# A transformer block on one core: memory attention's rows kept on chip, norms beside the last product, sums kept for the tail

## The chip, the core and the metric

One core of a Trainium2 chip runs the whole program in one launch. TensorE (PE) multiplies and transposes, VectorE (DVE), ScalarE (ACT) and GpSimd (POOL) do the elementwise work, SyncE (SP) issues most transfers, and 16 DMA engines carry them out. The metric is the device time of one execution in microseconds; the kernel before has three timed runs and one profiled execution.

## The reference, cut to what matters

`x` has 1024 rows of 1024. The block adds three terms to it, one after the other; a mixer with two kinds of sparse attention stands ahead of what the change touches.

```python
x = x + hybrid_mixer(rms_norm(x, norm1_g), ...)            # its last product is o @ w_out
x = x + memory_xattn(rms_norm(x, norm2_g), mem, ...)
x = x + square(relu(rms_norm(x, norm3_g) @ w_ff_in)) @ w_ff_out

def memory_xattn(h, mem, ...):                             # 4 heads of 128, 256 memory rows
    q = rms_norm(h @ w_xq); k = rms_norm(m @ w_xk); v = m @ w_xv
    o = softmax(q k^T * 128 ** -0.5) v                     # [1024, 512]
    return o @ w_xo
```

## The kernel before

**Tiles.** The 1024 rows are eight tiles of 128. A product needs its left operand transposed, features on the partitions. Most products split an operand into a high and a low part of a rounded format (`split_w`, L248, and `split_ps`, L242) and add three products; others take whole float32 operands, and such a product has two records in the trace.

**Stages.** `project` makes the projections of tiles 0 to 3 and then 4 to 7. After that two streams are mixed by `together` (L114): `attend`, the sparse attention tile by tile, and `fill` (L1219), which holds all other work: the second half of the projections, `memory` (keys and values of the memory), `between` for tiles 0 and 1, `between` for 2 and 3, `mlp` for tiles 0 to 3, and `between` for 4 and 5. When attention is done, `merge` (L1248) mixes what is left of `fill` with `between` for tiles 6 and 7, and `mlp_tail` (L1078) does the MLP of tiles 4 to 7.

**`between` (L919)** takes two tiles. It loads the attention outputs `o` and the rows of `x`, adds `o @ w_out` to them (four chunks of 256 columns, `gemm`, L322), normalizes and transposes the sums (`norm_T2`, L298: a square with row sums on ScalarE, a power on GpSimd, two scalings on VectorE, eight transposes on TensorE), and makes the queries in two chunks of 256 columns, two heads each. After a chunk, `memory_item` (L956) runs for both tiles in turns, a step of one and then of the other: norm of the queries, transposes, scores, softmax, transposes, values. Its result `o`, 128 rows by 256 columns, is written to a DRAM tensor `xo` (L1003). When both chunks are done, each tile's 512 columns are read back (L1009), transposed in one group of four (`to_T`, L276) into `xf`, and multiplied by `w_xo` in four chunks, each added to the sums. With `keep` the sums stay in SBUF (`x2s`), else they are written to `x2_dr` (L1017).

**The MLPs.** `mlp` (L1019) loads the sums of tiles 0 and 1 from `x2_dr`, normalizes and transposes all four tiles one after the other, and then goes through eight groups of 512 features. `mlp_tail` does the same for tiles 4 to 7; its first `G` = 2 groups run for tiles 4 and 5 before the norms of 6 and 7 (L1152). Tiles 4 and 5 come from `x2_dr` by `start` (L1086).

**Buffers.** `RINGS` (L38) gives the number of buffers of each tag in each pool. In `dn`, the pool of the middle, `b4` has four of 128x1024, `wraw` two (weights as loaded), `relu` two. `res` holds four rows of sums for the tail. A new tile takes a buffer that is free, and its first writer waits until the last reader of the old one is done. `psM`, where transposes land, has one buffer in the main part.

**Order.** Python makes the instructions in one order. A scheduler then orders each engine's queue by its own model of times (`TC_ARGS`, L83), so that instructions of the two streams alternate on every engine. Each engine, and SP with its transfers, works through its queue in that order: an instruction that waits holds up those behind it.

## Time and profile before

| | |
|---|---|
| timed runs, median of three (lowest, highest) | 1804.89 us (1802.81, 1807.52) |
| the profiled execution's own time | 1801.23 us |
| its span, first to last instruction | 1799.5 us |
| mean granted TensorE clock | 0.978 |
| busy: TensorE, its weight loads | 1697.9, 1460.7 us |
| busy: DVE, ACT, POOL | 948.0, 1070.5, 882.3 us |
| HBM read, written | 170.98, 20.97 MB |

A row of a timeline begins with its start in us from the span's first instruction and how long it took; `[1.82 <-DMA relu<-xo]` at its end says that the engine sat idle for 1.82 us before it, and what ended the wait. `psD<-whi,b` reads: written tile, read tiles. `psS`, `psPT` and `psPV` belong to attention in the main part and to the `between` of tiles 6 and 7 after it, `psD` and `psM` to `fill` and the tail. In the table by stage each engine has its busy time and its instructions, then come the granted TensorE clock as a share of full speed, the share of the DMA engines and the rate. SPq is SP's queue, with the time that issuing took. The program orders, of which the prediction speaks too, hold no times: they list each engine's instructions in the order of its queue, for the kernel before and the changed one.

### The profile page before, as it was taken

To read this page: it belongs to the slowest core of one execution; us is meant where nothing else is said; L and a number is where in the kernel's file an instruction comes from. 1 tells how busy PE (TensorE), PEld (TensorE's weight loads), DVE (VectorE), ACT (ScalarE), POOL (GpSimd) and SP (SyncE) were. 2 spreads that over 40 slices of the span, in tenths; PEclk is the share of its full clock that TensorE was granted. 3 is DMA by queue.
4 is the path that set the end of the run, shared out by engine and by line. 5 is a ranking of instruction groups with operands and counts; after the bars stand their busy time and mean duration, and the time that the engine had idled before them with its cause. 6 is when DMAs were issued, how large, how long until landed. Compare 5 with 4: busy or idle time off the path is not lost.

```text
span 1799.5 us, 28038 instructions
## 1 busy us (share of the span) xinstructions
PE 1697.9 (94%) x9326; PEld 1460.7 (81%) x9326; DVE 948.0 (53%) x2397; ACT 1070.5 (59%) x2687; POOL 882.3 (49%) x1025
## 2 busy tenths in 40 slices
PE   6989999899998889999998999999999889999998
PEld 6987988788787778778886888888978778888887
DVE  4556767667864675274564565656623552222223
ACT  4444885895697569845797457994512543333333
POOL 2356545564541446468476577563211444444445
PEclk9999999899999999999999999999999899999999
DMA  7334222654344311212222122225374642333333
GB/s 200 114 133 114 64 62 75 203 140 151 100 147 157 87 33 54 69 59 79 60 75 75 59 68 65 68 84 183 98 250 145 212 128 84 96 94 97 95 121 106
DMA packets 176977, 193.80 MB, mean 108 GB/s; under 512 B 25664, under 2 KB 144192, under 8 KB 176832
## 3 DMA queue, kind: packets, MB, share of 16 engines
q1 hardware_dynamic: 168896, 181.52, 33.3%
q0 software_dynamic: 7936, 10.49, 2.2%
q8 instruction: 74, 1.21, 0.3%
q14 instruction: 71, 0.58, 0.1%
HBM read 170.98 MB, written 20.97 MB: 107 GB/s over the span
## 4 chain that ended last, share of the span: by engine, by line
PE 69%; DMA 8%; DVE 8%; ACT 6%; POOL 4%; issue 4%; SPq 1%; POOLq 0%; DVEq 0%; ACTq 0%
PE psD L224 49%; PE psS L224 8%; PE psPV L224 4%; PE psPT L719 4%; ACT dmask L660 2%; POOL wlo L257 2%; PE psM L282 1%; DMA wraw<-in_w_ff_out_dram 1%; DMA xo<-relu 1%; POOL S L709 1%; DMA wraw<-in_w_ff_in_dram 1%; DMA qin<-q 1%; DMA x<-b 1%; DVE S L702 1%; ACT whi L252 1%
## 5 line engine op out<-in xcount | busy, mean ns | idle before, releaser
L257 POOL TENSOR_TENSOR wlo<-wraw,whi 128x512 fp32r<-128x512 f32 (+1 forms) x225 | 305.6, 1363 | 283.3 <-ACT whi L252 278.8
L224 PE MATMUL psD<-whi,h 128*128 128x512 f32 x1024 | 343.1, 403 | 10.3 <-DVE b L1148 5.4
L252 ACT ACTIVATE whi<-wraw 128x512 fp32r<-128x512 f32 x321 | 200.3, 627 | 208.2 <-PE psD L224 156.9
L224 PEld LDWEIGHTS psD<-whi,h 128*128 128x128 f32 x1024 | 194.0, 191 | 55.4 <-DVE b L1148 8.8
L224 PE MATMUL psD<-xh,whi 128*128 128x512 f32 (+1 forms) x576 | 211.3, 371 | 3.5 <-ACT relu L1051 2.6
L224 PE MATMUL psD<-xh,wlo 128*128 128x512 f32 (+1 forms) x576 | 211.6, 369 | 0.0
L224 PE MATMUL psD<-xl,whi 128*128 128x512 f32 (+1 forms) x576 | 211.0, 369 | 0.0
L224 PE MATMUL psD<-wlo,h 128*128 128x512 f32 x512 | 203.9, 399 | 0.6 <-POOL wlo L257 0.6
L224 PE MATMUL psD<-whi,xh 128*128 128x256 f32 (+1 forms) x704 | 194.2, 358 | 1.4 <-DVE Vd L244 0.9
L224 PE MATMUL psD<-wlo,xh 128*128 128x256 f32 (+1 forms) x704 | 191.2, 353 | 2.7 <-DMA wlo<-in_w_in_dram 2.3
L244 DVE TENSOR_TENSOR pl<-psPT,ph 128x512 fp32r<-128x512 f32 (+1 forms) x232 | 142.4, 620 | 62.0 <-ACT ph L243 61.0
L704 ACT ACTIVATE S<-S,mn 128x128 f32<-128x128 f32 (+7 forms) x192 | 142.8, 745 | 53.8 <-DVE mn L702 53.0
L243 ACT ACTIVATE ph<-psPT 128x512 fp32r<-128x512 f32 (+1 forms) x232 | 122.9, 540 | 65.3 <-PE psPT L719 57.9
L709 POOL TENSOR_SCALAR S<-S,sums,gi 128x640 f32<-128x640 f32 (+7 forms) x128 | 107.9, 852 | 108.7 <-DVE sums L707 81.2
L257 DVE TENSOR_TENSOR wlo<-wraw,whi 128x512 fp32r<-128x512 f32 (+1 forms) x96 | 82.9, 863 | 148.3 <-ACT whi L252 148.2
L224 PEld LDWEIGHTS psD<-wlo,xh 128*128 128x128 f32 x704 | 132.6, 194 | 14.3 <-DMA wlo<-in_w_in_dram 2.7
L224 PEld LDWEIGHTS psD<-whi,xh 128*128 128x128 f32 x704 | 133.2, 197 | 12.0 <-DVE Vd L244 1.5
L719 PE MATMUL psPT<-c_ident,S 128*128 128x128 f32 x816 | 132.5, 279 | 4.7 <-POOL S L709 2.3
L224 PEld LDWEIGHTS psD<-xh,whi 128*128 128x128 f32 x576 | 108.3, 188 | 21.5 <-ACT relu L1051 3.5
L224 PEld LDWEIGHTS psD<-xl,whi 128*128 128x128 f32 x576 | 108.2, 188 | 17.8
L224 PEld LDWEIGHTS psD<-xh,wlo 128*128 128x128 f32 x576 | 108.4, 188 | 17.5 <-POOL wlo L257 0.3
L224 PE MATMUL psS<-K,qh 128*128 128x384 f32 (+3 forms) x288 | 110.5, 387 | 4.4 <-DVE mn L702 3.7
(286 smaller groups left out, 3843.9 us busy)
## 6 DMA issues: line engine op xcount, KB each, us to landing
wraw<-in_w_ff_in_dram SPq DMA_DIRECT2D x40, 512.0 KB, 4.0
wraw<-in_w_ff_out_dram SPq DMA_DIRECT2D x40, 512.0 KB, 3.8
wraw<-in_w_ff_in_dram SPq DMA_DIRECT2D x64, 256.0 KB, 2.8
wraw<-in_w_ff_out_dram SPq DMA_DIRECT2D x64, 256.0 KB, 2.7
whi<-in_w_out_dram SPq DMA_DIRECT2D x32, 256.0 KB, 4.1
wlo<-in_w_out_dram SPq DMA_DIRECT2D x32, 256.0 KB, 4.3
wraw<-in_w_in_dram SPq DMA_DIRECT2D x24, 256.0 KB, 3.8
q<-st SPq DMA_DIRECT2D x12, 512.0 KB, 2.9
```

Source lines behind the costliest of these rows:

```text
L224: te.matmul(o, a, b, start=start, stop=stop)
L243: s.activation(hi, src, AF.Copy)
L244: v.tensor_tensor(lo, src, hi, op=ALU.subtract)
L252: s.activation(hi, raw, AF.Copy)
L257: (v if l == "v" else g).tensor_tensor(lo, raw, hi, op=ALU.subtract)
L282: te.transpose(pt[:, j, :], x_t[:, (c + j) * P:(c + j + 1) * P], ident)
L660: s.activation(mask, src, AF.Sign, bias=c, accum_out=over)
L702: v.tensor_tensor_reduce(out=dst, in0=sp, in1=m, scale=1.0, scalar=mn[:, 0:1] if i else 3e38, op0=ALU.add, op1=ALU.min, accum_out=low)
L704: s.activation(S, S, AF.Exp, bias=low, scale=-1.0, accum_out=sums[:, hh:hh + 1])
L709: g.tensor_scalar(Ss[hh], Ss[hh], sums[:, hh:hh + 1], 1.0 if gate is None else gate[:, hh:hh + 1], op0=ALU.mult, op1=ALU.mult)
L719: te.transpose(p2[:, j, hh, :], S[:, (c + j) * P:(c + j + 1) * P], ident)
```

## The change

Four edits. `memory_item` no longer writes `xo`: after a step's pause it transposes its 128x256 result at once, in two transposes, into a tile `xo` in SBUF (a buffer of `b4`), from which the `w_xo` product reads. `between` for tiles 2 and 3 gets a second stream, `pre_norms`, that alternates with its `w_xo` product: it loads the sums of tiles 0 and 1 from `x2_dr` (tile 1 in two halves that lie in `wraw`), normalizes and transposes them; `mlp` then only has tiles 2 and 3 to do, and loads tile 1 once more for the sums. If the pool `res` exists when `between` for tiles 4 and 5 comes to its `w_xo` product, its sums go to buffers of `res` and no longer through `x2_dr`. The tail's two rows of gains move to `res` and are loaded when that pool is opened.

```diff
...
     "p1": {"x4": 5, "st": 2, "relu": 4, "wraw": 4, "whi": 6, "wlo": 6, "c8": 4, "c4": 2, "kraw": 5, "pc": 2},
     "p2": {"x4": 5, "st": 1, "relu": 2, "whi": 4, "wlo": 4, "c8": 3, "c4": 1, "kraw": 4, "pc": 2},
     "dn": {"b4": 4, "h": 8, "relu": 2, "wraw": 2, "whi": 4, "wlo": 4},
-    "res": {"b4": 4},
+    "res": {"b4": 4, "g": 2},
     "d2": {"b4": 2, "h": 8, "relu": 2, "whi": 4, "wlo": 4},
-    "d3": {"g": 2, "h": 16, "relu": 2, "wraw": 4, "whi": 10, "wlo": 10},
+    "d3": {"h": 16, "relu": 2, "wraw": 4, "whi": 10, "wlo": 10},
 }
 PSUMS = {"p1": {"D": 4, "M": 3, "C": 1}, "main": {"S": 2, "PT": 2, "PV": 1, "D": 2, "M": 1}}
 TAGS = {"p1": ("D", "M", "C"), "p2": ("D", "M", "D"), "dn": ("D", "M"), "d2": ("S", "PT"), "d3": ("D", "M")}
...
     KX = [[dr.tile([P, 2, 256], F32R, tag=f"KX{a}{c}", name=f"KX{a}{c}") for c in range(2)] for a in range(2)]
     VX = [[dr.tile([P, 2, 256], F32R, tag=f"VX{a}{c}", name=f"VX{a}{c}") for c in range(2)] for a in range(2)]
     x2_dr = [dr.tile([P, DM], F32, tag=f"x2{t}", name=f"x2{t}") for t in range(NT)]
-    xo_dr = [dr.tile([P, 512], F32, tag=f"xo{t}", name=f"xo{t}") for t in range(NT)]
 
 
     ahead = {0: late["x"]}
...
             v.tensor_tensor(dst, pt, dst, op=ALU.add)
         return add_to
 
-    def between(pool, t0, nt, x2s, keep, res=None):
+    def between(pool, t0, nt, x2s, keep, res=None, then=None):
 
         o_of = []
         for t in range(nt):
...
         x2 = [ring(res or pool, "b4", [P, DM]) for t in range(nt)]
         for t in range(nt):
             nc.sync.dma_start(x2[t], I["x"][0, (t0 + t) * P:(t0 + t + 1) * P, :])
-        add_to = residual_add(x2)
-        four = [[(c * 256, 256)] for c in range(4)]
+        add_to, four = residual_add(x2), [[(c * 256, 256)] for c in range(4)]
         yield from gemm(pool, [lambda t, k: o_of[t][:, k, :]], 8, nt, W["w_out"], four, add_to)
         _, xf, xt_of = xT(pool, nt, True)
 
...
             yield 1.0
 
         kx, pts = [], {}
+        xo = ring(pool, "b4", [P, 4, nt * P])
 
         def consume_q(ci, t, pt):
             if t == 0:
...
             v.reciprocal(sums, sums)
             o = ring(pool, "relu", [P, 2, P])
             v.tensor_tensor(o, pv, sums[:, :, None].to_broadcast([P, 2, P]), op=ALU.mult)
-            nc.sync.dma_start(xo_dr[t0 + t][:, ci * 256:(ci + 1) * 256], o.rearrange("p h d -> p (h d)"))
+            yield 1
+            to_T(pool, o.rearrange("p h d -> p (h d)"), [xo[:, ci * 2:ci * 2 + 2, t * P:(t + 1) * P]], 2)
 
         yield from gemm(pool, xf, 8, nt, W["w_xq"], [[(0, 256)], [(256, 256)]], consume_q)
 
-        for t in range(nt):
-            o = ring(pool, "relu", [P, 512])
-            nc.sync.dma_start(o, xo_dr[t0 + t])
-            to_T(pool, o, [x[:, 0:4] for x in xt_of(t)], 4)
-            yield 0.5
-        yield from gemm(pool, xf, 4, nt, W["w_xo"], four, add_to)
+        if not keep and "res" in late:
+            kept = [ring(late["res"], "b4", [P, DM]) for t in range(nt)]
+            x2s.update((t0 + t, kept[t]) for t in range(nt))
+
+            def add_to(ci, t, pt):
+                cs = slice(ci * 256, (ci + 1) * 256)
+                v.tensor_tensor(kept[t][:, cs], pt, x2[t][:, cs], op=ALU.add)
+        last = gemm(pool, [lambda t, k: xo[:, k, t * P:(t + 1) * P]], 4, nt, W["w_xo"], four, add_to)
+        yield from alternate(last, then()) if then else last
         for t in range(nt):
             if keep:
                 x2s[t0 + t] = x2[t]
-            else:
+            elif t0 + t not in x2s:
                 nc.sync.dma_start(x2_dr[t0 + t], x2[t])
 
-    def mlp(pool, t0, nt, x2s):
+    def pre_norms(pool, made, x2s):
+
+        made["x"] = xT(pool, 4)
+        made["g"] = gain2(pool, W["norm3_g"])
+        xt_of = made["x"][2]
+        x2s[0] = ring(pool, "b4", [P, DM])
+        nc.sync.dma_start(x2s[0], x2_dr[0])
+        norm_T2(pool, x2s[0], made["g"], xt_of(0))
+        yield 1.0
+        halves_ = []
+        for c in range(2):
+            halves_.append(ring(pool, "wraw", [P, 512]))
+            nc.sync.dma_start(halves_[c], x2_dr[1][:, c * 512:(c + 1) * 512])
+        xs = xt_of(1)
+        ss = [small(pool, "nss", 1) for _ in range(2)]
+        for c in range(2):
+            s.activation(xs[0][:, c * 4:c * 4 + 4], halves_[c].rearrange("p (k c) -> p k c", c=P), AF.Square, accum_out=ss[c])
+        v.tensor_tensor(ss[0], ss[0], ss[1], op=ALU.add)
+        r = rsqrt_of(pool, ss[0], DM, 1, "n")
+        yield 0.5
+        for c in range(2):
+            xn = ring(pool, "relu", [P, 512])
+            v.scalar_tensor_tensor(xn, halves_[c], r[:, 0:1], made["g"][c], op0=ALU.mult, op1=ALU.mult)
+            to_T(pool, xn, [x[:, c * 4:c * 4 + 4] for x in xs], 4)
+            yield 0.5
+
+    def mlp(pool, t0, nt, x2s, made):
         x2 = []
         for t in range(nt):
             if t0 + t not in x2s:
...
                 nc.sync.dma_start(x2s[t0 + t], x2_dr[t0 + t])
             x2.append(x2s[t0 + t])
         add_to = residual_add(x2)
-        (xh, xl), _, xt_of = xT(pool, nt)
-        gb3 = gain2(pool, W["norm3_g"])
-        for t in range(nt):
-            norm_T2(pool, x2[t], gb3, xt_of(t))
+        (xh, xl), _, xt_of = made["x"]
+        for t in range(2, nt):
+            norm_T2(pool, x2[t], made["g"], xt_of(t))
             yield 1.0
 
         for f4 in range(8):
...
                                           x2[t][:, c * 512:(c + 1) * 512])
                     yield 2.6
 
-    def mlp_tail(pool, res, x2s, t0):
+    def mlp_tail(pool, res, x2s, t0, gb3):
 
         x2 = {}
         (xh, xl), _, xt_of = xT(pool, 4)
-        gb3 = [ring(pool, "g", [P, 512]) for _ in range(2)]
-        for i, gb in enumerate(gb3):
-            nc.sync.dma_start(gb, row(W["norm3_g"][i * 512:(i + 1) * 512]).to_broadcast([P, 512]))
 
         def start(t):
             if t0 + t in x2s:
...
     dn_pool = tc.tile_pool(name="dn", bufs=1, reuse_waits="tile")
     aw = aw_pool.__enter__()
     projected = []
+    late["x2s"] = {}
 
     def fill():
         for part in range(1, len(PARTS)):
...
         yield 1, PACES[1]
         yield from between(dn, 0, 2, {}, False)
         yield 3, PACES[2]
-        x2s = {}
-        yield from between(dn, 2, 2, x2s, True)
+        x2s, made = {}, {}
+        yield from between(dn, 2, 2, x2s, True, None, lambda: pre_norms(dn, made, x2s))
         yield 3, PACES[3]
-        yield from mlp(dn, 0, 4, x2s)
+        yield from mlp(dn, 0, 4, x2s, made)
         yield 5, PACES[4]
-        yield from between(dn, 4, 2, {}, False)
+        yield from between(dn, 4, 2, late["x2s"], False)
 
     rest = fill()
     together(attend(aw, st), rest, projected)
...
     sp_pool.__exit__(None, None, None)
     at_pool.__exit__(None, None, None)
     res_pool = tc.tile_pool(name="res", bufs=1, side="right", reuse_waits="tile")
-    res = res_pool.__enter__()
+    res = late["res"] = res_pool.__enter__()
+    gb3 = [ring(res, "g", [P, 512]) for _ in range(2)]
+    for i, gb in enumerate(gb3):
+        nc.sync.dma_start(gb, row(W["norm3_g"][i * 512:(i + 1) * 512]).to_broadcast([P, 512]))
     d2_pool = tc.tile_pool(name="d2", bufs=1, side="right", reuse_waits="tile")
     plan["w"] = PLAN_TAIL
     d2 = d2_pool.__enter__()
-    x2s = {}
+    x2s = late["x2s"]
     rest = (w for w in rest if not isinstance(w, tuple))
     merge((rest, REST), (between(d2, 6, 2, x2s, True, res), 45.0))
     dn_pool.__exit__(None, None, None)
     d2_pool.__exit__(None, None, None)
     with tc.tile_pool(name="d3", bufs=1, reuse_waits="tile") as d3:
-        mlp_tail(d3, res, x2s, 4)
+        mlp_tail(d3, res, x2s, 4, gb3)
     res_pool.__exit__(None, None, None)
     ctx.close()
 
```

## The prediction, made before the result was known

> **What bounds the kernel now.** I read the page's busy times first, then its chain of work, then the busy times by stage.
>
> ```profile
> PE 1697.9 (94%) x9326; PEld 1460.7 (81%) x9326; DVE 948.0 (53%) x2397; ACT 1070.5 (59%) x2687; POOL 882.3 (49%) x1025
> PE 69%; DMA 8%; DVE 8%; ACT 6%; POOL 4%; issue 4%; SPq 1%; POOLq 0%; DVEq 0%; ACTq 0%
> ```
>
> TensorE is the bound: busy 94% of the span and 69% of the chain. An edit that leaves its products alone (the program orders of both kernels hold 8460 products, of the same sizes) can only win the rest: time in which TensorE sits idle, and time at a lowered clock. The stages say where these are. I cut them at the places where the two program orders meet or part.
>
> ```profile
> core 0: us, PE busy (x) PEld busy (x) DVE busy (x) ACT busy (x) POOL busy (x), PEclk, DMA share, GB/s
> 473.00:568.00 95.00, 89.20 (x519) 78.75 (x518) 57.62 (x162) 79.91 (x216) 35.77 (x52) 0.98 0.46 142
> 568.00:592.00 24.00, 18.32 (x91) 14.27 (x91) 17.27 (x59) 15.41 (x44) 3.10 (x5) 0.93 0.29 101
> 592.00:686.00 94.00, 82.66 (x505) 71.33 (x505) 70.61 (x208) 62.59 (x154) 40.02 (x53) 0.96 0.20 58
> 686.00:760.00 74.00, 71.62 (x351) 58.88 (x350) 27.72 (x65) 64.09 (x159) 44.47 (x48) 0.98 0.22 67
> 760.00:1306.00 546.00, 532.06 (x2832) 451.23 (x2832) 313.62 (x746) 372.67 (x827) 325.67 (x330) 0.99 0.27 82
> 1306.00:1323.00 17.00, 14.43 (x64) 12.06 (x62) 2.62 (x6) 2.36 (x7) 3.17 (x6) 0.80 0.90 280
> 1323.00:1355.00 32.00, 31.50 (x160) 27.83 (x161) 10.07 (x30) 5.87 (x16) 1.94 (x3) 1.00 0.68 215
> 1355.00:1407.00 52.00, 44.63 (x250) 39.06 (x249) 25.70 (x64) 18.63 (x44) 11.02 (x14) 0.92 0.63 196
> 1407.00:1465.00 58.00, 57.59 (x365) 52.57 (x364) 25.37 (x37) 29.19 (x60) 30.13 (x32) 0.98 0.48 143
> 1465.00:1800.00 335.00, 320.52 (x1487) 264.52 (x1485) 95.67 (x130) 112.69 (x193) 151.42 (x128) 0.99 0.33 101
> ```
>
> A stage's loss is its length less the busy time, plus its length times the missing clock. 592 to 686 (end of the second `between`, norms of the MLP) loses 11.3 + 3.8 = 15.1 us. 1306 to 1323 (attention's end) loses 2.6 + 3.4 = 6.0 us. 1355 to 1407 (memory attention of tiles 6 and 7 and the tail's first norms) loses 7.4 + 4.2 = 11.5 us. The change works in these three and at one wait near 507. Up to 473 the order of the products is the same, and from 1465 on (the tail's MLP) it is the same again: nothing is to be won there.
>
> **The change part by part. (a) The detour through DRAM.** The four waits that it leaves on TensorE:
>
> ```profile
> 509.14 0.63 PE L282 MATMUL psM<-c_ident,relu 128*128 128x128 f32 x4 [1.82 <-DMA relu<-xo]
> 626.84 0.63 PE L282 MATMUL psM<-c_ident,relu 128*128 128x128 f32 x4 [3.32 <-DMA relu<-xo]
> 1363.46 0.66 PE L282 MATMUL psM<-c_ident,relu 128*128 128x128 f32 x4 [1.26 <-DMA relu<-xo]
> 1423.93 0.63 PE L282 MATMUL psPT<-c_ident,relu 128*128 128x128 f32 x4 [0.30 <-DMA relu<-xo]
> ```
>
> The bracket is the idle time and what ended it: 1.82 + 3.32 + 1.26 + 0.30 = 6.7 us over the four calls of `between`. The 24 transfers go; the 32 transposes of 128x128 stay 32, and ScalarE copies 16 half-size tiles in place of 8. In the changed order 19 to 40 products stand, in the two calls beside attention, between the last product of an item and the transposes of its result, so nothing is late in their place. First term, for the wait at 507: **-1.8**. The other three lie in the stages below and are counted there. One thing follows: `xo` sits in a `b4` buffer, so that the loads of tile 3's attention output wait for the first `w_xo` product to end, where they now trickle in early. The order leaves 25 products before their first use; I take 0, with 4 us as the far end (the wait of 3.32 is the nearest row for a transfer that comes late).
>
> **(b) Norms beside `w_xo`.** Now the MLP's eight groups of transposes stand with attention alone beside them, after all 32 `w_xo` products. In the changed order four of the eight stand among the `w_xo` products, and the first MLP product comes 93 products sooner. I take half of the stage's loss: **-7.6**, from 0 to -15.1. Not all of it, since the norms of tiles 2 and 3 still wait for the last `w_xo` sums.
>
> [...]
>
> **(c) The tail.** Tiles 4 and 5 stay in `res`: their trip through DRAM goes, and their norms and first features now stand beside the memory attention of 6 and 7, which today runs bare:
>
> ```profile
> 1402.16 1.22 PE L224 MATMUL psS<-h 128*128 128x256 f32 x4 [1.89 <-DVE h L244]
> 1405.38 0.48 PE L989 MATMUL psPT<-c_ident,relu 128*128 128x128 f32 x1 [1.99 <-ACT relu L983]
> ```
>
> In the changed order 75 feature products stand between the first scores of tiles 6 and 7 and their last `pv`. Of the 11.5 us I leave 3.5 (four norms now come at once on ScalarE and VectorE): **-8.0**, from 0 to -11.5. That tiles 4 and 5 really are kept is seen in the order: two writes of `x2_dr` are left of four.
>
> **(d) Attention's end, the other way.** The chunk of queries that fills TensorE today after attention's last product has mostly moved before it: 8 of its 16 products are left.
>
> ```profile
> 1306.13 0.28 PE L224 MATMUL psPV<-pl,Vd 128*128 128x256 f32 x1
> 1307.43 0.44 PE L224 MATMUL psD<-h 128*128 128x128 f32 x2 [1.02 <-ACT h L243]
> 1308.57 3.93 PE L224 MATMUL psD<-h 128*128 128x128 f32 x22
> 1312.30 2.02 PE L224 MATMUL psD<-whi,xh 128*128 128x256 f32 x4
> 1318.24 1.03 PE L224 MATMUL psD<-whi,xh 128*128 128x256 f32 x4
> 1323.08 1.10 PE L224 MATMUL psS<-whi,b 128*128 128x256 f32 x4 [1.22 <-DMA whi<-in_w_out_dram]
> 1302.31 2.47 SPq L925 DMA_DIRECT2D b<-o  x5
> 1308.45 0.58 SPq L733 DMA_DIRECT2D o<-oc  x1
> 1309.08 5.55 SPq L925 DMA_DIRECT2D b<-o  x11
> 1314.73 0.85 SPq L929 DMA_DIRECT2D b<-in_x_dram  x2
> 1316.89 0.38 SPq L273 DMA_DIRECT2D whi<-in_w_out_dram  x1
> ```
>
> Today, counted from 1306.1: last output written at +2.3, 11 loads of it in 5.55 us (0.50 each; 5 went earlier, and the 11 stood behind that write on SP, which issues in order), `w_out` asked for at +10.8, its first product at +17.0. In the changed queue of SP, all 16 loads of `o` stand behind four `w_xo` loads whose buffers are freed only by those last 8 query products. These take 8 x 0.45 = 3.6 us (a product is two records here; four records in 0.86 to 1.03 us), so the queue moves on at about +5, the 16 loads take 8.1, `w_out` is asked for at +13.1 and arrives 6.2 later: +19.3. TensorE has 3.6 us of queries and 12 scores, 12 transposes and 24 narrow products (0.18 at the lowered clock by the row of 22), some 10 us in all. So 9.3 us idle and again 3.4 of clock, 12.7 against 6.0: **+6.7**, from +2 (the loads go faster) to +12.
>
> **(e) The long stretch between.** Every edit also reshuffles what comes after it: 686 to 1306 holds the same products in another mix. Today it loses 3.9 + 19.4 = 23.3 us, by its two rows above. In the changed order attention is up to 78 products further behind, and its longest pause, for a top-k mask, has 108 MLP products alone in it, not 132. No row prices another mix; I take **0**, with 5 us to each side, about a fifth of the loss.
>
> Sum: -1.8 - 7.6 - 8.0 + 6.7 + 0 = -10.7. The profiled execution took 1801.23 us (span 1799.5), 3.7 less than the median of the three timed runs, 1804.89. So 1790.5 for a profiled execution like that one, and **1794** for the median.
>
> **The rivals.**
>
> *Both gaps close.* If (b) and (c) win nearly all (-13, -11) and (d) costs 3, the sum with (a) is -23: 1782. For it: today's gaps there are latencies, and the new order puts products into them. Against it: (d).
>
> *The gain moves.* (b) wins 3, since tiles 2 and 3 wait as before, (c) 5, (a) nothing, as the loads of tile 3 come late, and (d) costs 9: +1, 1806. For it: in 1306 to 1323 DMA is already at 0.90 of its engines, so earlier requests need not land earlier. [...]
>
> *Slower: the MLP starts without weights.* `pre_norms` holds tile 1 in both `wraw` buffers of `dn` until its norm is done, so the MLP's first four weight loads can start only then.
>
> ```profile
> 638.83 0.38 SPq L262 DMA_DIRECT2D wraw<-in_w_ff_in_dram  x1
> 643.96 5.83 SPq L262 DMA_DIRECT2D wraw<-in_w_ff_in_dram  x2
> 656.16 0.37 SPq L262 DMA_DIRECT2D wraw<-in_w_ff_in_dram  x1
> 686.05 0.40 PE L224 MATMUL psD<-xh,whi 128*128 128x512 f32 x1
> L252 ACT ACTIVATE whi<-wraw 128x512 fp32r<-128x512 f32 x321 | 200.3, 627 | 208.2 <-PE psD L224 156.9
> wraw<-in_w_ff_in_dram SPq DMA_DIRECT2D x64, 256.0 KB, 2.8
> L257 POOL TENSOR_TENSOR wlo<-wraw,whi 128x512 fp32r<-128x512 f32 (+1 forms) x225 | 305.6, 1363 | 283.3 <-ACT whi L252 278.8
> ```
>
> Today the first goes 47 us before the first MLP product. From the first request to the fourth it takes 17.3 us, and with landing (2.8) and the two splits (0.6 and 1.4) 22 us until the fourth is ready. In the changed order about 90 products lie between the norm of tile 1 and the first MLP product, 17 us at this stage's 94 us for 505 records, and some 8 us more until the fourth load's weights are used: 25 us for 22. From the point where four loads take over 25 us TensorE waits. At half of today's pace, 44 us, that is +19 and some 2 us of lowered clock, which eats the -10.7 and leaves +10: 1815.
>
> **How the numbers follow.** A measurement of this kernel tells about 0.3% from no change, 5.4 us: below 1799.5 is faster, above 1810.3 slower. The forecast (1788 to 1799) has a chance of 0.44, both gaps closed 0.22, the gain moved 0.21, slower 0.13. So faster 0.66, same 0.21, slower 0.13. The range reaches from the first rival to a little past the second, 1780 to 1808, and leaves out the last and the tips. It takes in (b) at 0 alone or (d) at +12 alone, not both.
>
> **What would show it.** In the profile after: no `xo` transfers and none of the four waits; the stage from the second `between`'s queries to the first MLP product shorter, with TensorE's loss near 7 us and no wait of MLP products for `whi` or `wlo`; a wait of `psS<-whi,b` for `w_out` just after attention's last product, some 19 us after it, with the clock near 0.5 around it; the memory attention of tiles 6 and 7 among `psD<-xh` products, with waits under 1 us; the stretch from the tail's third norm on as long as now. I am wrong if that `w_out` wait is short, if the eight norm groups still wait, or if the stretch between 760 and 1306 changes by more than the three together.

## The result, and the profile after

The changed kernel takes **1789.01 us** (median of four, 1787.41 to 1791.38) against 1803.85 us for the kernel before (median of four, 1800.25 to 1807.52): a ratio of **0.9919, 95% interval 0.9895 to 0.9942**. The forecast was 1794, in a range of 1780 to 1808. The profiled execution took 1789.06 us, its span is 1787.3, and the mean clock 0.980 (0.978 before). Two of the ten executions of one experiment below (`xo` alone) fell into a slow state (1929.62 and 9447.61 us); its numbers are those of the other eight.

The busy times of the whole execution, kernel after:

```profile
PE 1694.9 (95%) x9326; PEld 1460.5 (82%) x9326; DVE 953.0 (53%) x2398; ACT 1071.7 (60%) x2697; POOL 885.5 (50%) x1025
```

TensorE has the same number of records and 3 us less of busy time in a span that is 12.2 us shorter: 9 of the 12 us that went are idle time. (The medians are 14.8 us apart. The profiled execution of the kernel before, 1801.23, lies 2.6 under its median.)

Busy times by stage, kernel after. The columns are those of the table in the prediction: length, then busy time of PE, PEld, DVE, ACT and POOL with their instructions, clock, DMA share, GB/s.

```profile
474.50:566.70 92.20, 89.61 (x514) 79.81 (x513) 56.70 (x162) 79.29 (x217) 36.09 (x52) 0.96 0.44 138
566.70:598.80 32.10, 26.86 (x151) 22.99 (x152) 21.70 (x73) 19.00 (x52) 7.02 (x11) 0.95 0.33 103
598.80:664.90 66.10, 59.59 (x353) 52.47 (x351) 52.02 (x147) 40.98 (x102) 31.30 (x38) 0.92 0.21 63
664.90:747.20 82.30, 80.77 (x442) 68.89 (x441) 45.86 (x111) 75.18 (x187) 52.10 (x58) 1.00 0.20 63
747.20:1301.60 554.40, 540.16 (x2882) 455.75 (x2882) 318.63 (x752) 382.63 (x854) 326.21 (x331) 0.99 0.26 83
1301.60:1320.90 19.30, 14.06 (x70) 11.74 (x68) 7.28 (x23) 5.50 (x16) 3.53 (x6) 0.77 0.81 248
1320.90:1365.20 44.30, 44.30 (x197) 38.55 (x198) 7.86 (x18) 3.28 (x7) 0.57 (x1) 0.95 0.42 137
1365.20:1382.90 17.70, 13.35 (x66) 10.82 (x65) 15.10 (x25) 11.94 (x24) 9.73 (x9) 0.90 0.79 247
1382.90:1454.30 71.40, 70.31 (x459) 64.51 (x459) 31.10 (x67) 32.58 (x76) 32.22 (x37) 1.00 0.44 140
```

Stages of two kernels compare only where both program orders have done the same products. Three such places serve from here on: the 2115th product in PE's program (the first query product of tiles 0 and 1), the 3564th (early in the MLP of tiles 0 to 3) and the 7056th (early in the tail's MLP). Up to the first the orders are identical, and from the third on too. I call what lies between them **stretch S** (second and first `between`, norms, start of the MLP) and **stretch T** (the rest of the MLP, attention's end, the tail's start). The same view, cut at these places, before and then after:

```profile
442.50:759.60 317.10, 291.15 (x1644) 248.41 (x1643) 195.31 (x557) 242.16 (x626) 140.01 (x184) 0.97 0.30 91
759.60:1488.70 729.10, 699.70 (x3749) 598.47 (x3748) 389.54 (x898) 436.44 (x963) 380.40 (x390) 0.98 0.35 106
```
```profile
443.40:747.30 303.90, 287.29 (x1644) 250.36 (x1643) 199.11 (x558) 235.60 (x612) 143.18 (x185) 0.97 0.30 93
747.30:1476.40 729.10, 701.28 (x3749) 596.62 (x3748) 390.89 (x899) 443.50 (x987) 380.27 (x389) 0.98 0.32 100
```

The record counts of PE are the same (1644 and 3749), so the lengths may be subtracted. **All of the gain lies in S: 317.1 to 303.9, -13.2 us. T is 729.1 in both.** With +0.9 ahead of S and +0.1 behind T that is the span's -12.2. So in these two profiles attention's end, the kept sums and the reshuffled middle come to nothing together, as they nearly did in the forecast (-8.0 + 6.7 + 0); and S gave more than its -1.8 - 7.6.

Two of the signs that the prediction named, in the timelines of the kernel after. First PE and SP at the start of the MLP (the rival in which it starts without weights):

```profile
663.62 0.63 PE L282 MATMUL psM<-c_ident,relu 128*128 128x128 f32 x4 [0.57 <-DVE relu L305]
664.93 0.50 PE L224 MATMUL psD<-xh,whi 128*128 128x512 f32 x1
```
```profile
636.62 6.37 SPq L262 DMA_DIRECT2D wraw<-in_w_ff_in_dram  x3
646.39 4.16 SPq L262 DMA_DIRECT2D wraw<-in_w_ff_in_dram  x2
```

These five loads of weights are out by 650.6, 14 us ahead of the first MLP product, which has no bracket: it waited for nothing. That rival did not come. Next, PE and then SP at attention's end:

```profile
1301.56 0.28 PE L224 MATMUL psPV<-pl,Vd 128*128 128x256 f32 x1
...
1313.79 4.93 PE L224 MATMUL psD<-h 128*128 128x128 f32 x22
1320.89 3.78 PE L224 MATMUL psS<-whi,b 128*128 128x256 f32 x8 [2.17 <-DMA whi<-in_w_out_dram]
```
```profile
1305.87 0.42 SPq L273 DMA_DIRECT2D wlo<-in_w_xo_dram  x1
1306.38 11.53 SPq L924 DMA_DIRECT2D b<-o  x16
1318.00 0.38 SPq L273 DMA_DIRECT2D whi<-in_w_out_dram  x1
```

All 16 loads of `o` stand behind the four `w_xo` loads, and `w_out` is asked for only then. Its first product starts 1320.89 - 1301.56 = 19.3 us after attention's last one.

### The profile page after: what moved, and what is told of

It is laid out like the page before. It is cut to its first block, busy times and chain, and to the rows that moved or that the text cites. A ratio compares the mean times of both kernels' runs of the same rounds, so it can differ in the third digit from the quotient of the medians.

```text
span 1787.3 us, 27995 instructions
## 1 busy us (share of the span) xinstructions
PE 1694.9 (95%) x9326; PEld 1460.5 (82%) x9326; DVE 953.0 (53%) x2398; ACT 1071.7 (60%) x2697; POOL 885.5 (50%) x1025
## 4 chain that ended last, share of the span: by engine, by line
PE 56%; ACT 4%; DVE 3%; DMA 3%; issue 2%; POOL 2%; SPq 1%; POOLq 0%; ACTq 0%; DVEq 0%
PE psD L224 41%; PE psS L224 7%; PE psPV L224 4%; PE psPT L718 3%; ACT dmask L659 1%; POOL wlo L257 1%; DMA wraw<-in_w_ff_in_dram 1%; SPq L924 1%; DMA whi<-in_w_out_dram 1%; PE psM L282 1%; PE psPT L605 0%; ACT whi L252 0%; DVE b L1173 0%; DMA b<-o 0%; ACT tkt L661 0%
## 5 line engine op out<-in xcount | busy, mean ns | idle before, releaser
L224 PE MATMUL psD<-wlo,xh 128*128 128x256 f32 (+1 forms) x608 | 166.5, 350 | 3.1 <-DMA wlo<-in_w_in_dram 2.6
L224 PE MATMUL psD<-whi,xh 128*128 128x256 f32 (+1 forms) x608 | 166.7, 350 | 1.5 <-DVE Vd L244 1.2
L257 DVE TENSOR_TENSOR wlo<-wraw,whi 128x512 fp32r<-128x512 f32 (+1 forms) x96 | 78.8, 820 | 146.2 <-ACT whi L252 146.0
L224 PEld LDWEIGHTS psD<-wlo,xh 128*128 128x128 f32 x608 | 114.7, 195 | 12.2 <-DMA wlo<-in_w_in_dram 3.0
L224 PEld LDWEIGHTS psD<-whi,xh 128*128 128x128 f32 x608 | 114.6, 195 | 10.1 <-DVE Vd L244 1.5
L224 PEld LDWEIGHTS psD<-xl,whi 128*128 128x128 f32 x576 | 108.1, 188 | 16.9
L224 PEld LDWEIGHTS psD<-wlo,h 128*128 128x128 f32 x512 | 97.0, 190 | 21.3 <-POOL wlo L257 2.9
```

The costliest lines, as they stand in the source:

```text
L224: te.matmul(o, a, b, start=start, stop=stop)
L257: (v if l == "v" else g).tensor_tensor(lo, raw, hi, op=ALU.subtract)
```

## The experiments

The question is which edit made the 13 us in S, and why T gave nothing. Theories, as the expectations name them:

- **A**: each edit acts in its own stage and they add up: the norms win most of S, `xo` a little, the kept sums 4 us in the tail that attention's end eats. The wait at attention's end is set by the order of SP's queue.
- **B**: the `xo` edit makes the whole gain. **C**: the kept sums are worth their 8 us, and something else hides it.
- **D** (formed after the first four runs): the norms need the `xo` edit, through a buffer. **E** (formed last): what the tail still loses is four norms at once.

All kernels together; each ratio is against the kernel before, timed beside it, with its 95% interval. S and T are from the profiled execution. "Order" gives two facts of PE's program order: how many of the eight groups of norm transposes of the MLP stand ahead of the last `w_xo` product of tiles 2 and 3, and the place of the first MLP product. (The expectations count single transposes between the first and the last `w_xo` product, 4, 12, 16 or 20 of them; four of these belong to `xo`, so that they are 0, 2, 3 or 4 groups of the norms.)

| kernel | median, us | ratio | S, us | T, us | order |
|---|---|---|---|---|---|
| before | 1803.85 | 1 | 317.1 | 729.1 | 0, 3217 |
| norms alone | 1813.18 | 1.0051 (1.0035 to 1.0066) | 318.4 | 739.3 | 0, 3217 |
| sums alone | 1805.53 | 1.0009 (0.9997 to 1.0020) | 320.4 | 732.8 | 0, 3217 |
| norms and sums | 1815.98 | 1.0069 (1.0049 to 1.0089) | 322.1 | 738.9 | 0, 3217 |
| xo alone | 1796.62 | 0.9960 (0.9944 to 0.9976) | 308.6 | 738.0 | 2, 3181 |
| xo and sums | 1793.66 | 0.9946 (0.9926 to 0.9966) | 303.2 | 734.3 | 2, 3181 |
| xo and norms | 1793.13 | 0.9947 (0.9929 to 0.9964) | 301.8 | 734.2 | 4, 3124 |
| after | 1789.01 | 0.9919 (0.9895 to 0.9942) | 303.9 | 729.1 | 4, 3124 |
| after, again | 1791.55 | 0.9923 (0.9907 to 0.9940) | 304.6 | 731.5 | 4, 3124 |
| norms alone, w_xo from b4 | 1802.79 | 0.9999 (0.9984 to 1.0014) | 308.8 | 734.4 | 3, 3155 |
| after, o by whole tiles | 1781.10 | 0.9874 (0.9852 to 0.9897) | 299.5 | 723.2 | 4, 3122 |
| the same, w_out earlier | 1782.33 | 0.9886 (0.9868 to 0.9904) | 302.4 | 722.6 | 4, 3122 |
| after, REST 1000 | 1794.02 | 0.9942 (0.9922 to 0.9962) | 303.4 | 736.0 | 4, 3124 |
| o by whole tiles, REST 1000 | 1786.92 | 0.9903 (0.9883 to 0.9923) | 303.2 | 725.9 | 4, 3122 |

How far a single S or T can be trusted: ahead of S every kernel has the identical order, and yet that part took from 441.6 to 446.7 us; behind T it took 310.4 to 310.9 in all. S of the two kernels with the order 2, 3181 differs by 5.4. And a profiled execution is not always near its kernel's median: with norms and sums it is 4.5 us over it, with `xo` alone 4.2 over, with the norms and `w_xo` from `b4` 5.4 under. So differences under 5 us between two rows are read only where several rows agree.

**xo alone.** Of the change, only this:

```diff
+        xo = ring(pool, "b4", [P, 4, nt * P])
...
-            nc.sync.dma_start(xo_dr[t0 + t][:, ci * 256:(ci + 1) * 256], o.rearrange("p h d -> p (h d)"))
+            yield 1
+            to_T(pool, o.rearrange("p h d -> p (h d)"), [xo[:, ci * 2:ci * 2 + 2, t * P:(t + 1) * P]], 2)
...
-        yield from gemm(pool, xf, 4, nt, W["w_xo"], four, add_to)
+        last = gemm(pool, [lambda t, k: xo[:, k, t * P:(t + 1) * P]], 4, nt, W["w_xo"], four, add_to)
```

> Memory attention's rows are transposed at once; the norms of tiles 0 and 1 and the sums of 4 and 5 are as before. The sum by parts (theory A: each part acts in its own stage, the norms win most, xo a little, the sums of 4 and 5 nothing on balance): the four waits for xo, 1.8 + 3.3 + 1.3 + 0.3 = 6.7 us, go at most, and some of them come back as other waits: -2 to -5 against the kernel before. The rival (theory B: the xo edit makes the whole gain, because it lets the scheduler put every product of memory attention elsewhere): -12 to -15, as much as the whole change. Attention's end: 49 program products between attention's last product and the first w_out product, the loads of o straight behind the last write, so no longer than 17 us there.

Measured 0.9960, -7.2 us: more than the sum by parts allowed, half of what B wanted. S is 8.5 shorter, beyond the four waits for `xo` (6.7 in all, 5.1 of it in S); T is 9 longer. Its order shows where S can gain: two norm groups stand among the `w_xo` products, where none stood, though nobody touched the norms. Attention's end took 17.1 us, at the edge of the 17 expected. (Its profiled execution took 1800.78, so its S and T together are some 4 us long.)

**Norms alone.** Of the change, only the second stream beside `w_xo`:

```diff
-        yield from between(dn, 2, 2, x2s, True)
+        x2s, made = {}, {}
+        yield from between(dn, 2, 2, x2s, True, None, lambda: pre_norms(dn, made, x2s))
```

> Norms of tiles 0 and 1 beside w_xo; xo through DRAM and the sums of 4 and 5 as before. Theory A: the stage from the second between's queries to where both orders have done the same MLP products wins most of the 10 us seen in the changed kernel: -7 to -10 against before. Theory B (xo makes the gain): within 3 us of before.

Measured 1.0051, +9.2 us: **theory A falls.** The edit that was to win most of S is slower by itself and leaves S where it was (318.4 for 317.1). B, which wanted it within 3 us of before, misses it too. Its order answers at once: no norm group ahead of the last `w_xo` product and the first MLP product at place 3217, exactly as before. Asking for the norms earlier moved none of them ahead of the last `w_xo` product.

**Sums alone.**

```diff
+            def add_to(ci, t, pt):
+                cs = slice(ci * 256, (ci + 1) * 256)
+                v.tensor_tensor(kept[t][:, cs], pt, x2[t][:, cs], op=ALU.add)
```

(with the buffers `kept` in `res`, and the gains there).

> Sums of 4 and 5 kept, gains in the tail's room; xo and the norms as before. Theory A (the tail's win of 4 us is eaten by a longer bubble at attention's end, which this edit makes together with xo): between -5 and +3 against before; here fewer of the 16 loads of o stand behind w_xo loads, so the bubble is not longer than 18 us. Theory C (the tail is worth 8 us as forecast, and only the bubble and the reshuffled middle hide it): -6 to -9.

Measured 1.0009, the interval reaching from -0.5 to +3.6 us. C is out; without the `xo` edit the sums win nothing. Attention's end stayed at 16.9 us.

**O by whole tiles.** On the changed kernel:

```diff
-    oT_dr = [[dr.tile([P, P], F32, ...) for c in range(8)] for t in range(NT)]
+    oT_dr = [dr.tile([P, 8, P], F32, ...) for t in range(NT)]
...
-            for c in range(8):
-                nc.sync.dma_start(o[:, c, :], oT_dr[t0 + t][c])
+            nc.sync.dma_start(o, oT_dr[t0 + t])
```

> The changed kernel, with attention's output of a tile in one DRAM tile, so that it is loaded in 1 transfer of 512 KB in place of 8 of 64 KB, everywhere. Theory A (the bubble at attention's end is 16 issues on SP, 11.5 us, ahead of the w_out loads): w_out is asked for some 10 us sooner, the first w_out product comes at +10 to +13 us after attention's last product in place of +19.3, and the kernel is 5 to 9 us faster than the changed kernel. Rival (the bytes bound it: the DMA engines are busy 0.81 in that stage): +17 to +19, and less than 2 us of difference.

Measured 1781.10, ratio 0.9874: 8 us faster than the changed kernel. Its interval lies clear of the row "after, again" (0.9907 to 0.9940) and touches that of the first measurement (0.9895 to 0.9942) by its edge. SP and PE at attention's end, o by whole tiles:

```profile
1301.15 1.10 SPq L927 DMA_DIRECT2D b<-in_x_dram  x2
1302.34 3.63 SPq L923 DMA_DIRECT2D b<-o  x2
1306.06 0.39 SPq L273 DMA_DIRECT2D whi<-in_w_out_dram  x1
```
```profile
1299.24 0.28 PE L224 MATMUL psPV<-pl,Vd 128*128 128x256 f32 x1
...
1313.90 3.33 PE L224 MATMUL psS<-whi,b 128*128 128x256 f32 x7 [3.33 <-DMA whi<-in_w_out_dram]
```

From the first request of these loads to the end of the last one it is 3.63 us, where 16 loads took 11.53. Not all of that is issuing. These are waits of SP's queue at attention's end (us in total, times, longest), first kernel after, then o by whole tiles:

```profile
SPq L924 <- DMA b<-o: 1.8, 2, 1.2
SPq L924 <- DMA b<-in_x_dram: 0.9, 1, 0.9
SPq L924 <- DMA wlo<-in_w_xo_dram: 0.8, 2, 0.4
SPq L924 <- DMA whi<-in_w_xo_dram: 0.8, 2, 0.4
```
```profile
SPq L923 <- DMA o<-oc: 2.7, 1, 2.7
```

In the kernel after, 4.3 of the 11.53 us are seven waits for earlier transfers to land, each for the one eight places ahead in the queue. The other 7.2 us are the 16 issues, 0.45 each. With whole tiles, 2.7 of the 3.63 us are the wait for the write of attention's last output.

`w_out` is asked for 6.8 us after attention's last product, not 16.4, and its first product starts at +14.7, not +19.3. Of the 9.6 us by which it is asked for sooner, 7.9 are these loads; the other 1.7 come from the four `w_xo` loads, which now stand ahead of attention's last product. The first product is later than the +10 to +13 expected, since the transfer now takes 7.8 us from its request and not 2.9. From 1306 to 1314 the DMA engines moved 385 to 403 GB/s, where they moved 231 from 1312 to 1318 in the kernel after: this speaks for bytes in front of it, as the rival had it. So both seem to have had a part; the queue had the larger one. The end of attention accounts for 4.7 of the 8 us. The `between` of tiles 4 and 5 has its 16 loads ahead of `w_out` in the same way, but nothing was won there. The waits for `w_out` in it, kernel after and then whole tiles:

```profile
PE psD L224 <- DMA whi<-in_w_out_dram: 3.2, 1, 3.2
```
```profile
PE psD L224 <- DMA whi<-in_w_out_dram: 3.3, 2, 1.8
```

From the 3564th product to attention's last one both take the same (554.3 and 554.1 us). What is left of the 8 us lies mostly in S (303.9 to 299.5), which one profile doesn't tell from noise.

**Theory D.** The order of the norms-alone kernel sent me to its buffers. The normed rows of the MLP go to the pair `xh`, `xl` of pool `dn`. Before, `w_xo` reads its left operand from `xf`, which has the tag `xh` too. So the first writer of the normed rows, the square on ScalarE, must wait for the last `w_xo` product, wherever the norms are asked for. The `xo` edit moves that operand to a `b4` buffer, and `xh` is free once the queries are made. To tell the buffer from the detour through DRAM:

**Norms alone, w_xo from b4.** As norms alone, `xo` through DRAM and back, but

```diff
-            to_T(pool, o, [x[:, 0:4] for x in xt_of(t)], 4)
+            to_T(pool, o, [xo[:, :, t * P:(t + 1) * P]], 4)
...
-        last = gemm(pool, xf, 4, nt, W["w_xo"], four, add_to)
+        last = gemm(pool, [lambda t, k: xo[:, k, t * P:(t + 1) * P]], 4, nt, W["w_xo"], four, add_to)
```

with `xo` in a buffer of `b4`.

> The norms alone on the kernel before, xo still through DRAM and back, but its rows are then transposed into a buffer of their own (b4) and not into xh; sums as before. So only what holds xh differs from the norms-alone kernel, which was 0.5% slower than before at 1813 us. In the order 16 transposes (4 there) now stand ahead of the last w_xo product and the first MLP product comes 62 products sooner. Theory D (xh is what tied the norms): the stage from the second between's w_xo to the common MLP product is 5 to 9 us shorter than with the norms alone, and the kernel at 1803 to 1808. Rival (what the norms alone lose lies elsewhere, in the wait for xo or in the middle): within 3 us of 1813.

Measured 1802.79 against 1813.18, -10 us by an edit that saves no work and no transfer, a little past the expected 1803; the two intervals lie clear of each other. ScalarE's writers of `xh` in the two kernels (duration min/median/max in ns, first and last start in us), norms alone and then w_xo from b4:

```profile
L301 ACT ACTIVATE xh<-b x3: 1051/1061/1062, 657.6 to 664.2; 128x1024 fp32r<-128x1024 f32 x3
L1036 ACT ACTIVATE xh<-wraw x2: 618/629/640, 659.1 to 660.5; 128x512 fp32r<-128x512 f32 x2
```
```profile
L301 ACT ACTIVATE xh<-b x3: 1059/1060/1086, 631.1 to 656.0; 128x1024 fp32r<-128x1024 f32 x3
L1038 ACT ACTIVATE xh<-wraw x2: 614/626/638, 632.1 to 634.0; 128x512 fp32r<-128x512 f32 x2
```

With the norms alone, the first square (tile 0) starts at 657.6, right behind the last `w_xo` product, which starts at 657.0; with the buffer freed it starts at 631.1, 22 us ahead of that product (653.7). The last four `w_xo` products of the norms-alone kernel, and ScalarE's row, whose wait ends with a `psD` product:

```profile
656.52 1.03 PE L224 MATMUL psD<-wlo,xh 128*128 128x256 f32 x4
657.58 1.06 ACT L301 ACTIVATE xh<-b 128x1024 fp32r<-128x1024 f32 x1 [0.30 <-PE psD L224]
```

S falls from 318.4 to 308.8. Both stretches of each, norms alone first:

```profile
445.40:763.80 318.40, 291.47 (x1643) 249.49 (x1642) 196.22 (x558) 242.94 (x628) 141.76 (x184) 0.96 0.31 94
763.80:1503.10 739.30, 708.34 (x3750) 603.61 (x3749) 390.33 (x898) 437.58 (x963) 375.04 (x390) 0.97 0.34 105
```
```profile
441.70:750.50 308.80, 286.00 (x1644) 247.54 (x1643) 198.57 (x556) 239.12 (x616) 143.31 (x186) 0.98 0.32 99
750.50:1484.90 734.40, 703.35 (x3750) 599.61 (x3749) 390.95 (x900) 439.14 (x975) 376.87 (x388) 0.97 0.34 105
```

The profiled execution of the second, 1797.37, is the fastest of its twelve, so its S and T are some us short; the medians, the orders and the starts of the squares don't hang on it. Nor does S over the whole table: the four kernels in which `w_xo` reads `xh` have 317.1 to 322.1 us, the ten in which it doesn't 299.5 to 308.8.

**D is shown:** the buffer tied the norms, not the detour. Three more runs ask what it leaves for each edit.

**Xo and norms** (the changed kernel, sums of 4 and 5 through DRAM).

```diff
-        if not keep and "res" in late:
-            kept = [ring(late["res"], "b4", [P, DM]) for t in range(nt)]
```

> The changed kernel with the sums of 4 and 5 through DRAM again, so xo and norms. Theory D (the norms need the xo edit: the MLP's normed rows lie in the buffer xh, which w_xo read until its last product, so that norms alone moved nothing in the order; together with xo, 20 of the 32 transposes stand ahead of the last w_xo product, 4 before): the stage from the second between to the common MLP product is as in the changed kernel, some 10 us shorter than before. The sums edit alone gave +0.1% against before; if it is worth nothing here too, this kernel stands within 3 us of the changed one, at 1786 to 1792. Rival (the sums win 8 us as forecast, once xo is there): 1795 to 1799.

Measured 1793.13, between the two expectations. S is as short as in the changed kernel (301.8), so D holds. By the medians the sums are worth 2 to 4 us on top (1789.01 and 1791.55 with them), in T (734.2 without, 729.1 and 731.5 with), but the intervals of these ratios overlap.

**Xo and sums** (the changed kernel, all four norms in `mlp`).

```diff
-        yield from between(dn, 2, 2, x2s, True, None, lambda: pre_norms(dn, made, x2s))
+        yield from between(dn, 2, 2, x2s, True)
...
-        for t in range(2, nt):
+        for t in range(nt):
```

> The changed kernel without the norms edit, so xo and sums. In its order 12 of 32 transposes stand ahead of the last w_xo product (20 in the changed kernel, 4 before) and the first MLP product comes 57 products later than in the changed kernel. Theory D: most of the norms' 10 us came with xo already, the edit itself is worth 3 to 6 us on top: 1792 to 1796. Rival (the order of the norms doesn't matter, the run without the xo wait alone is what counts): within 2 us of the changed kernel.

Measured 1793.66, as D said: by the medians the norms edit is worth 2 to 5 us on top of `xo`, again with intervals that overlap. In S it can't be told from noise (303.2 without; 303.9 and 304.6 with).

The two pairs with and without the sums (`xo` alone, `xo` and sums; `xo` and norms, after) show where the sums act. From the first `w_out` product of tiles 6 and 7 to the end of T it was 159.4 and is 154.2 us, 160.2 and 155.5: 5 us less in both. Ten of these products now stand at attention's end, which is 2 us longer for them (17.1 to 19.1, 17.4 to 19.3). So some 3 us of the forecast's 8 are left.

**Norms and sums** (the changed kernel, `xo` through DRAM and into `xh`).

```diff
-        xo = ring(pool, "b4", [P, 4, nt * P])
...
+            nc.sync.dma_start(xo_dr[t0 + t][:, ci * 256:(ci + 1) * 256], o.rearrange("p h d -> p (h d)"))
```

> The changed kernel with xo through DRAM again, so norms and sums without the xo edit. Theory D (without xo the buffer xh ties the norms): in the order 4 of 32 transposes stand ahead of the last w_xo product and the first MLP product has the place that it had before; the stage around them as before, and the whole as the norms alone (+0.5%) and the sums alone (+0.1%) put together: 1808 to 1816. Rival (the parts add: 1789 plus the 7 us that xo alone is worth): 1794 to 1798.

Measured 1815.98, as D said, 20 us from adding up. So the edits don't add: `xo` alone is -7 us, and with the other two there it is worth 1815.98 - 1790 = some 26; norms and sums alone are +9 and +2 (the +2 can't be told from 0), and behind `xo` they are worth a few us each.

**W_out earlier**, on the kernel with whole tiles:

```diff
             o_of.append(o)
+            if res and t == 0:
+                begun = list(weights(pool, [None], 8, W["w_out"], four[0]))
```

> The changed kernel with attention's output loaded by whole tiles (which gave 1781), and the first four w_out loads of tiles 6 and 7 asked for between the loads of tile 6 and of tile 7. Theory A (the queue's order and bytes ahead of w_out set the bubble; there w_out was asked for at +6.8 us after attention's last product and its first product came at +14.7): w_out is asked for 2 us sooner with 512 KB less ahead of it: first product at +11 to +13, 1778 to 1781. Rival (the rest of the bubble is memory attention's own chain of waits, or the x loads ahead): no difference beyond 1 us.

Measured 1782.33 beside 1781.10, and the first product at 1312.83 - 1299.30 = +13.5 us, 1.1 sooner: a miss for A. `w_out` was asked for 3.0 us sooner (at +3.8), so most of that was lost again on the way, while the DMA engines moved 379 to 397 GB/s (1306 to 1313). That points to the bytes under way and not to the queue; whether it is the two loads of `x` ahead wasn't tried.

**After, again, and REST 1000.** The changed kernel once more, and the changed kernel with another `REST`, the number by which `merge` mixes what is left of tiles 4 and 5 with tiles 6 and 7:

```diff
-REST = 70.0
+REST = 1000.0
```

> The changed kernel itself, timed beside the three others: 1786 to 1792 if the first four executions stand for it. Its stretch from the common MLP product to the place where both orders meet again is 705 to 709 us, as in its first profile (707.0), if that stretch hangs on the order; a spread of several us there would mean that the reshuffled middle can't be told from noise.

> The changed kernel with REST 1000 in place of 70, so that what is left of tiles 4 and 5 after attention is put ahead of tiles 6 and 7, and two of the eight norm groups stand among the w_out products. Theory E (what the tail still loses, 4.4 idle + 4.1 clock from the last w_out product to the first tail features, is four norms at once, with VectorE busy 15.1 of 17.7 us, where it was busy 7.9 of 44.3 in the w_out stage ahead): the tail's loss falls by 3 to 6 us, 1783 to 1787. Rival (the loss is the chain of tiles 6 and 7 alone, norm to queries to scores, whatever 4 and 5 do): within 2 us of the changed kernel.

The changed kernel came out at 1791.55; its ratio (0.9923) repeats the first. The stretch that was expected at 705 to 709 us took 709.2, and T was 729.1 and 731.5: a spread of over 2 us for one order. REST 1000 is 1794.02, no gain, against E. The view by stage shows what became of the earlier norms, REST 1000 and then after (from the first `w_out` product to the tail's first features; then from where the orders were to meet to the 7056th product):

```profile
1324.10:1381.90 57.80, 53.81 (x237) 46.07 (x237) 21.52 (x36) 13.42 (x25) 9.66 (x9) 0.90 0.58 190
1453.70:1482.40 28.70, 22.68 (x96) 18.12 (x95) 12.05 (x18) 8.04 (x14) 5.32 (x5) 0.88 0.14 43
```
```profile
1320.90:1382.90 62.00, 57.65 (x261) 49.37 (x262) 22.97 (x43) 15.22 (x30) 10.30 (x10) 0.93 0.53 168
1454.30:1476.40 22.10, 19.21 (x84) 15.30 (x83) 11.01 (x16) 7.68 (x14) 8.10 (x6) 0.92 0.32 103
```

The first place still loses 4.0 us of idle time (57.80 - 53.81; 4.35 after), and the second, where tiles 6 and 7 are normed, now loses 6.0 where it lost 2.9, with a lower clock (0.88 for 0.92). There the transposes wait for VectorE's normed rows (`xl`) 4.7 us in all, 2.1 in the kernel after. So the norms of 4 and 5 seem to be no cover to be had twice: with their features gone ahead, tiles 6 and 7 are normed with less beside them.

**Whole tiles and REST 1000.**

> The kernel with attention's output loaded by whole tiles (1781), and REST 1000. In its order only one norm group moves ahead of the last w_out product. Theory E: 1 to 3 us less, 1778 to 1780. Rival (chain of tiles 6 and 7 alone): 1780 to 1782.

Measured 1786.92, 6 us over whole tiles alone by the medians (the intervals overlap), past the rival too. It is the same exchange: the wait for `xl` in that place is 4.8 us, 2.1 without REST 1000. The best kernel of the study is the one with whole tiles, 1781.10.

## Why the prediction came out, point by point

The number is near and the sign right; two of its reasons were not, and that the sum came out near is partly luck. S gave 3.8 us more than its two terms. T gave 0 for a forecast of -1.3, but of two terms that were both put at nearly twice their size and cancelled. (The program holds 8458 products, not 8460; nothing hangs on it.)

- **(a) The detour, -1.8.** Right in size: from the fork of the orders to the first query work of tiles 2 and 3, 94.6 us became 92.2 (-2.4). No `xo` transfer is left. Tile 3's loads of `o` came late nowhere: no product waits for them. But its real effect was missed, the freed `xh`.
- **(b) Norms beside `w_xo`, -7.6.** S lost 13.2 in all, 10.0 of it from 598.8 to 747.2 (601.2 to 759.6 before), so the term was somewhat small. The idle time there is 6.5 + 1.5 = 8.0 us, against 11.3 + 2.4 = 13.7 (84.8 - 73.46 and 73.6 - 71.22, the profile of before cut at 601.2, 686.0 and 759.6). The other 4.3 of the 10.0 us are busy time: the same records took 140.36 us in place of 144.68, which a count of idle time and clock doesn't foresee. **The step that failed is the attribution:** "In the changed order four of the eight stand among the `w_xo` products" was read off the order of the whole change, and put down to the edit that asks for them there. Alone that edit leaves the order up to the last `w_xo` product and S as they were, since the squares wait for the buffer `xh` until the last `w_xo` product; the `xo` edit alone takes S from 317.1 to 308.6, and with the sums to 303.2. The right term for (b) was 0 without (a), and for (a) most of both. The clock did not rise: 0.92 in 598.8 to 664.9 (0.96 before, in 601.2 to 686.0), so TensorE's loss there is 6.5 + 5.3 = 11.8, not near 7.
- **(c) The tail, -8.0.** Mis-sized: 1320.9 to 1454.3 loses 0.0 + 4.4 + 1.1 idle and 2.2 + 1.8 of clock, 9.5, where 1323 to 1465 lost 13.7 by the prediction's rows (0.5 + 7.4 + 0.4 and 4.2 + 1.2). So -4.2. I left 3.5 for four norms at once; they take more, here:

```profile
1367.45 0.63 PE L282 MATMUL psM<-c_ident,relu 128*128 128x128 f32 x4 [1.22 <-DVE relu L305]
1373.18 0.63 PE L282 MATMUL psM<-c_ident,relu 128*128 128x128 f32 x4 [0.78 <-DVE xl L244]
1375.89 1.19 PE L224 MATMUL psS<-whi,xh 128*128 128x256 f32 x4 [2.08 <-ACT xh L286]
```

  4.1 of the 4.35 us idle in 1365.2 to 1382.9 are these three, with VectorE busy 15.1 of 17.7 us.
- **(d) Attention's end, +6.7.** The place was right. The moment, +19.3 to the tenth, was luck: two errors of 3.3 us cancel. `w_out` was asked for at +16.4, not +13.1 (the 16 loads took 11.53 us and not 8.1, 4.3 of it waits of the queue for earlier transfers), and arrived in 2.9, not 6.2. The clock near 0.5 came (0.50 from 1312 to 1320.9), but the wait for `w_out` itself is 2.17 us. The price was mis-sized: 5.2 idle and 4.4 of clock, 9.7 against 6.0, so +3.7. The sum had TensorE busy for some 10 us there, and it was busy for 14.1, in part because the products that fill that time ran at the lowered clock themselves (22 narrow ones in 4.93 us at 0.50, against 3.93 us at 0.73 before); so they left 5.2 us idle, not 9.3.
- **(e) The long middle, 0.** 747.2 to 1301.6 has 14.2 us idle at 0.99, 759.6 to 1306.1 had 13.9 at 0.99: 0, in these profiles. Yet T is 734 to 739 in the six kernels that have part of the change with `xo` or norms in it. Kept sums alone stand at 732.8, the whole change at 729.1 and 731.5. Why T grows by up to 10 us with `xo` or the norms alone **stays open**, and part of it may be noise. With the norms alone the same 3750 records are busy 8.6 us longer (708.34 for 699.70) at a clock of 0.97, so there it looks like the clock and the mix more than new waits. With `xo` alone it is idle time more than busy time (35.3 us idle for 29.4). From the 3564th product to attention's last one the two kernels with `xo` and without the norms edit took 561.5 and 560.9 us, the four with the order of the whole change 554.3 to 558.1. No run took it apart.

Of the rivals, the MLP without weights needed tile 1's two buffers to be held too long; the first weights were asked for 28 us before the first MLP product (636.6 for 664.9). "Both gaps close" was right for S, not for the tail. What no rival said is that one edit is the condition of another; a kernel with the norms alone would have ended beyond the range, at 1813.

## What to carry to other kernels

When a change asks for work earlier, look up which buffer the work writes and who reads that buffer last: if the two meet in one tag, the work may not move (the first square stood at 657.6 us with `xh` held, at 631.1 with it freed), and an edit that only seemed to save a transfer may be the one that frees it. Read off the program order of each edit alone, not only of the whole, before putting a term down to an edit. And look at what stands on the queue ahead of a load that everything waits for: the issues, and the waits for earlier transfers to land (7.2 and 4.3 of the 11.53 us here). Loading attention's output in one piece per tile and not in eight was worth 8 us, half as much as this change, and 4.7 of them lie in one place.

## What the runs showed of the hardware that was not expected

**The clock at attention's end.** Kernel after, in the columns of the table by stage:

```profile
1306.40:1312.00 5.60, 3.39 (x18) 2.15 (x18) 3.23 (x12) 2.92 (x10) 2.81 (x5) 1.00 1.01 312
1312.00:1318.00 6.00, 5.66 (x26) 5.48 (x27) 1.80 (x3) 0.85 (x2) 0.00 (x0) 0.50 0.79 231
```

The clock is 1.00 from 1306.4 to 1312 and 0.50 from 1312 to 1320.9. TensorE is busy for 3.39 of the 5.60 us ahead of the drop and for 5.66 of the 6.00 us behind it. What the clock goes by is not shown. From 1301.6 to 1320.9, 4.4 us of clock were lost (19.3 us at 0.77) beside 5.2 us of idle time; the prediction had 3.4 and 9.3.

**Small loads on one queue.** In the kernel after, 16 loads of 64 KB took 11.53 us on SP's queue, where 11 of them took 5.55 before. The difference is not in the issues: 4.3 of the 11.53 us are waits for transfers eight places ahead to land, and without them an issue took 0.45 us (0.50 before). The same bytes in two loads took 3.63 us, 2.7 of it a wait for a write to land.
